# Down projection of a gated FFN: 8 of its 22 inner tiles as seven products over pairs of output tiles instead of eight

## The chip, the cores and the metric

One kernel runs on one core of a Trainium2 chip. The metric is the device time of one launch in microseconds (us). The core has five engines with a queue each: PE (matrix products, with its weight loads shown as PEld), DVE and ACT (element-wise work), POOL and SP (which here issues most transfers). Each engine works through its own queue in order; they wait for each other by semaphores.

## The reference, cut to what matters

The reference is one layer of a hybrid decoder: three gated token mixers, then a ConvFFN, over 1024 prompt tokens and 32 sample tokens, all float32. Only its last product is changed:

```
up = rmsnorm(x, g_pre_f) @ w_up                        # 1024 -> 2 x 2816
fa, fb = split(causal_dwconv(up, ffn_prev, conv_f_w, conv_f_b))
x = x + rmsnorm((silu(fa) * fb) @ w_down, g_post_f)    # 2816 -> 1024
```

`w_down` has 2816 rows, which are 22 inner tiles of 128, and 1024 columns, which are 8 output tiles of 128.

## The kernel before, in words

Everything is held transposed: a tile has 128 features on the partitions and the T = 1056 tokens along the free axis. A float32 operand is split into a high part (rounded to the PE's float32r type, by a copy on ACT, L91) and a low part (the rest, by a subtraction on DVE, L97). A product of two such operands takes three PE passes: high by high, high by low, low by high (`mm`, L100). So an inner tile times an output tile costs three passes for each chunk of tokens.

**The plain scheme** (`products`, L195). For an output tile, up to four inner tiles are multiplied for three chunks of 352 tokens; each chunk accumulates in one of five PSUM banks that are taken in turn (three called mm, two called wb), and is then evacuated. With four inner tiles that is 3 chunks x 4 tiles x 3 passes = 36 passes of 352 columns.

**The seven-product scheme** (`strassen`, L229, after Strassen and Winograd) is there already, for most of the up projection (j = 3 to 20) and for the gates. A pair of output tiles by eight inner tiles is a 2 x 2 block product: the inner tiles are two halves of four, and the tokens are two halves of 528, each again cut so that the parts p = 0, 1 pair columns of 264. Seven products of four inner tiles (names "11", "21", "T2", "T1", "T3", "T4", "22") take the place of eight; each is 2 parts x 4 tiles x 3 passes = 24 passes of 264 columns, so a pair has 168. The left operands are sums of weight blocks, made on DVE by `add_pair` (L169: four additions, L94, and seven splits). The right operands are sums of activation blocks, which have to be made once and are then used for all pairs. The products accumulate in banks called mm (X), wb (W) and aux (V).

**The down projection** comes last. The activations silu(fa) * fb are stored by tile to DRAM (`y2d`) as the up projection makes them, and come back by `load_y` (L1162): one transfer of 528 KB into the low slot, a copy on ACT into the high slot, a subtraction on DVE. Their slots are rows of Y and H, two large buffers of 16 rows each; until the down projection H holds the right operand of the up projection and Y its sums. The list `DOWN` (L33) cuts inner tiles 0 to 15 into four segments of four; `down` (L1168) runs a segment as eight plain units, one for each output tile, and adds into M (the first segment copies, on ACT; the later ones add, on DVE). After each unit it can load one more activation tile. Inner tiles 16 to 21 (`LAST` = 16 on) are done in a last stage by token chunks, which the final norm follows; that stage is not touched.

**Weights.** Every block of 128 x 512 weights is one transfer into a `raw` buffer (three of them), then a split into `wh` and `wl` (three each, so a split waits until PE is done with the split three before it). `make` keeps this three items ahead of PE, `load` four. In the pair scheme the blocks go to `xraw` buffers, which during the up projection are pieces of M.

**What sets the order.** PE's instructions stand in the order in which the program is written. In the down projection the other engines' queues are laid out by a scheduler that simulates the program, so their order is not in the source.

Of the kernel before, what the change touches and what calls it, by code (L numbers as in the profile page):

```python
# [9 lines left out]
F32 = mybir.dt.float32  # L10
F32R = mybir.dt.float32r
AF = mybir.ActivationFunctionType
ALU = mybir.AluOpType
# [4 lines left out]
P = 128  # L18
# [3 lines left out]
T = SEQ + NS  # L22
# [3 lines left out]
NFF = 22  # L26
# [3 lines left out]
NEG = -1e30  # L30
SCALE = 0.125
LAST = 16
DOWN = [(0, 4), (4, 8), (8, 12), (12, 16)]  # L33
PLAIN = 3
NC1 = 8 * 4 + 6 + 32 + 8 + 2
NCST = NC1 + 132 + 44
# [3 lines left out]
def body(tc, i, o):  # L40
    nc = tc.nc
    act, dve, pool, pe = nc.scalar, nc.vector, nc.gpsimd, nc.tensor
    top = ExitStack()
    with top, tc.manual_schedule(engines={mybir.EngineType.PE}):
        open_pool = lambda st, name, **kw: st.enter_context(tc.tile_pool(name=name, **kw))
# [12 lines left out]
        Y = fixed.tile([P, 16, T], F32R, name="Y")  # L58
        M = fixed.tile([P, 8 * T], F32, name="M")
        M8 = M.rearrange("p (k t) -> p k t", k=8)  # L60
        Yf = Y.rearrange("p s t -> p (s t)")
        x2d = dram.tile([P, 8, T], F32, name="x2d")
        y2d = dram.tile([P, NFF, T], F32, name="y2d")
# [20 lines left out]
        def cc(c):  # L84
            return slice(c * CW, (c + 1) * CW)

        def f32(ap):
            return ap.bitcast(F32)

        def copy(out, in_):  # L90
            act.activation(out, in_, AF.Copy)  # L91

        def tt(out, a, b, op, eng=dve):
            return eng.tensor_tensor(out, a, b, op=op)  # L94

        def sub(out, a, b, eng=dve):
            eng.tensor_tensor(out, a, b, op=ALU.subtract)  # L97
# [24 lines left out]
        xraw, limit = [None], [1 << 30]  # L122
# [33 lines left out]
        def add(src, nk, eng, where=None):  # L156
            for k0 in range(0, nk, 4):
                n = min(4, nk - k0)
                at = len(loads)
                loads.append((src[:, k0 : k0 + n, :], n, False))  # L160

                def fn(at=at, n=n, k0=k0):
                    raw, raws[at] = raws[at], None
                    to = where() if callable(where) else where
                    return split(raw, n, to and [t[:, k0 : k0 + n, :] for t in to], eng)

                items.append((at, n, fn))
# [54 lines left out]
        HC = 264  # L222

        def halves(p):

            one, two = ((0, 1), (3, 2))[p]
            return slice(one * HC, (one + 1) * HC), slice(two * HC, (two + 1) * HC)
# [49 lines left out]
        def unit(*args, **kw):  # L277
            for _ in products(*args, **kw):
                pass
# [77 lines left out]
        for j in range(2, NFF):  # L357
# [2 lines left out]
                continue  # L360
            for part in range(2):
                add(i["wu"][j + NFF * part], 8, dve)
        for g0, g1 in DOWN:
            for n in range(8):
                add(i["wd"][n, :, g0:g1, :], g1 - g0, dve)
        lastw = len(items)
        Hf = H.rearrange("p s t -> p (s t)")
        nl = (NFF - LAST) * P
        rest_of = [Yf[:, 12 * T + nl * q :][:, :nl] for q in range(5)] + [Hf[:, nl * q :][:, :nl] for q in range(11)]
        for n in range(8):  # L370
            add(i["wd"][n, :, LAST:NFF, :], NFF - LAST, dve,
                [rest_of[2 * n + h].rearrange("p (k m) -> p k m", m=P) for h in range(2)])
# [654 lines left out]
        with us:  # L1027
# [70 lines left out]
            def act_pair(j):  # L1098
                za = conv(*tile_of(j, 0))
                zb = conv(*tile_of(j, 1))  # L1100
                act.activation(za, za, AF.Silu)
                tt(za[:, :SEQ], za[:, :SEQ], zb[:, :SEQ], ALU.mult)
                tt(four(za[:, SEQ:T]), rest(za), rest(zb), ALU.mult)
                nc.scalar.dma_start(y2d[:, j, :], za[:, :T])
# [47 lines left out]
                    pass  # L1152
                act_pair(j)

            slots = [(Y[:, k], Y[:, 4 + k]) for k in range(4)]
            slots += [(Y[:, 8 + k], Y[:, 12 + k]) for k in range(4)]
            slots += [(H[:, k], H[:, 4 + k]) for k in range(4)]
            slots += [(H[:, 8 + k], H[:, 12 + k]) for k in range(4)]
            slots += [(Y[:, k], Y[:, 6 + k]) for k in range(6)]
            act_slot = lambda k: slots[k]  # L1160

            def load_y(k):  # L1162
                h, l = slots[k]
                nc.sync.dma_start(f32(l), y2d[:, k, :])
                copy(h, f32(l))
                sub(l, f32(l), f32(h))

            def down(k0, k1, then):  # L1168
                then = iter(then)
                for n in range(8):  # L1170
                    def evac_d(c, ps):
                        m = M8[:, n, cc(c)]
                        if k0 == 0:
                            copy(m, ps)
                        else:
                            tt(m, ps, m, ALU.add)
                    unit(k1 - k0, lambda k: act_slot(k0 + k)[0], lambda k: act_slot(k0 + k)[1], evac_d)
                    for k in [k for k in [next(then, None)] if k is not None]:
                        load_y(k)

            j = NFF - 1
            for part in range(2):
                for q, _ in enumerate(up_unit(j, part, CHUNKS)):
                    if not part and q < 4:
                        load_y(q)
            act_pair(j)
            nc.sync.dma_start(o["fx"], fx)
        for (k0, k1), then in zip(DOWN, (range(4, 8), range(8, 12), range(12, 16), range(16, 22))):
            down(k0, k1, then)


        with tc.tile_pool(name="pl", bufs=1) as pl:
# [162 lines left out]
```

## Time and profile before

| | |
|---|---|
| three timed runs | 1462.86 us median (1462.71 to 1464.74) |
| the profiled execution | 1468.9 us; its span, first to last instruction, 1467.1 us |
| PE's busy share of the span | 98% |
| DVE, ACT, POOL | 61%, 45%, 16% |
| mean granted PE clock | 0.987 |

The page's slices show PE at nine tenths or more from the second to the second-last slice. A busy PE says little alone, because passes overlap and their ends are modelled; what a pass costs is read from the distance between starts.

### The profile page before, as it was taken

Reading aid. Unit: us, or ns where it says so; the run is one execution under the profiler, and the core shown is the slowest. Engines: PE = TensorE matmul, PEld = TensorE weight load, DVE = VectorE, ACT = ScalarE, POOL = GpSimd, SP = SyncE. Lnnn points to the kernel's source line nnn. Section 1 sums busy time; section 2 is a strip of 40 time slices with the busy share of each in tenths; the row PEclk is TensorE's granted clock in tenths of the full one; section 3 lists DMA queues with packets and bytes.
Section 4 is the critical chain, followed back from the end, with each engine's and each line's share of the span. In section 5 each row is a group of like instructions: output and inputs, shape, how many; then the busy total and the mean of one; then the engine's idle time right before and its main releaser. Section 6 shows DMA issues by size and latency. Waiting matters only on the chain.

```text
span 1467.1 us, 25813 instructions
## 1 busy us (share of the span) xinstructions
PE 1438.9 (98%) x10211; PEld 1428.3 (97%) x10211; DVE 901.2 (61%) x1623; ACT 659.4 (45%) x1346; POOL 235.2 (16%) x319
## 2 busy tenths in 40 slices
PE   7999999999999999999999999999999999999997
PEld 7999999999999989999999999999999999999997
DVE  6665444325777546755678787777877782454546
ACT  6344444445766322243446455445544574121333
POOL 0000000013455215510002221222212210000000
PEclk7999999999999999999999999999999999999998
DMA  5223233211111136642232312222222274231215
GB/s 196 93 96 110 97 102 103 100 48 37 30 30 37 60 119 210 192 159 84 83 111 73 102 66 74 81 87 83 65 79 74 78 258 141 72 103 45 86 42 151
DMA packets 77817, 141.40 MB, mean 96 GB/s; under 512 B 8240, under 2 KB 34800, under 8 KB 77680
## 3 DMA queue, kind: packets, MB, share of 16 engines
q1 hardware_dynamic: 64256, 110.05, 23.8%
q10 hardware_dynamic: 13440, 29.70, 5.4%
q8 instruction: 80, 1.31, 0.4%
q14 instruction: 41, 0.34, 0.1%
HBM read 105.58 MB, written 35.16 MB: 96 GB/s over the span
## 4 chain that ended last, share of the span: by engine, by line
PE 91%; DVE 4%; ACT 2%; issue 2%; DMA 1%; SPq 0%; POOL 0%; ACTq 0%; POOLq 0%; DVEq 0%
PE mm L100 55%; PE wb L100 21%; PE aux L100 13%; DVE M L94 1%; PE sp L100 1%; ACT M L731 1%; PE aux L744 1%; DVE Y L97 1%; DVE M L416 1%; DVE M L725 0%; DMA M<-in_x 0%; DVE H L97 0%; DMA cst<-in_cst 0%; DVE M L604 0%; ACT Y L91 0%
## 5 line engine op out<-in xcount | busy, mean ns | idle before, releaser
L100 PE MATMUL mm<-Y,wh 128*128 128x264 f32 (+1 forms) x1824 | 363.8, 294 | 0.0
L100 PE MATMUL mm<-H,wh 128*128 128x352 f32 (+1 forms) x1568 | 354.4, 313 | 1.5 <-DVE Y L97 0.9
L100 PEld LDWEIGHTS mm<-Y,wh 128*128 128x128 f32 x1824 | 292.4, 188 | 0.0
L100 PE MATMUL mm<-Y,wl 128*128 128x264 f32 (+1 forms) x912 | 269.1, 295 | 0.0
L100 PEld LDWEIGHTS mm<-H,wh 128*128 128x128 f32 x1568 | 261.4, 188 | 2.5 <-PE aux L100 1.1
L100 PE MATMUL mm<-H,wl 128*128 128x352 f32 (+1 forms) x784 | 243.4, 311 | 0.0
L100 PEld LDWEIGHTS mm<-Y,wl 128*128 128x128 f32 x912 | 171.6, 188 | 0.0
L91 ACT ACTIVATE wh<-M 128x512 fp32r<-128x512 f32 x126 | 79.5, 631 | 152.8 <-PE aux L100 67.6
L100 PE MATMUL wb<-H,wh 128*128 128x264 f32 (+1 forms) x720 | 147.7, 298 | 0.0
L100 PEld LDWEIGHTS mm<-H,wl 128*128 128x128 f32 x784 | 147.2, 188 | 0.0
L91 ACT ACTIVATE wh<-raw 128x512 fp32r<-128x512 f32 (+1 forms) x98 | 58.2, 595 | 170.8 <-PE mm L100 111.7
L1092 DVE SCALAR_TENSOR_TENSOR cz<-U,cst,cz 128x1072 f32<-128x1072 f32 x88 | 113.7, 1329 | 10.9 <-ACT cz L1090 10.9
L100 PEld LDWEIGHTS wb<-H,wh 128*128 128x128 f32 x720 | 116.4, 188 | 0.0
L100 PE MATMUL mm<-H,Y 128*128 128x352 f32 x624 | 108.7, 333 | 1.0 <-DVE H L97 0.9
L100 PE MATMUL wb<-H,wl 128*128 128x264 f32 (+1 forms) x360 | 107.2, 298 | 0.0
L97 DVE TENSOR_TENSOR wl<-M,wh 128x512 fp32r<-128x512 f32 x126 | 86.3, 685 | 33.0 <-ACT wh L91 32.9
L100 PEld LDWEIGHTS mm<-H,Y 128*128 128x128 f32 x624 | 104.1, 194 | 2.1 <-DVE H L97 1.5
L97 DVE TENSOR_TENSOR wl<-xraw,wh 128x512 fp32r<-128x512 f32 x70 | 48.4, 692 | 80.6 <-ACT wh L91 80.2
L94 DVE TENSOR_TENSOR M<-M 128x512 f32<-128x512 f32 (+1 forms) x88 | 69.5, 789 | 27.8 <-DMA M<-in_wu 27.1
L94 DVE TENSOR_TENSOR M<-mm,M 128x352 f32<-128x352 f32 (+3 forms) x79 | 39.5, 505 | 76.6 <-PE mm L100 76.5
L97 DVE TENSOR_TENSOR wl<-raw,wh 128x512 fp32r<-128x512 f32 (+1 forms) x72 | 52.3, 729 | 51.9 <-ACT wh L91 51.9
L91 ACT ACTIVATE U<-mm 128x264 f32<-128x264 f32 (+4 forms) x199 | 63.8, 342 | 44.9 <-PE mm L100 42.5
(222 smaller groups left out, 2598.1 us busy)
## 6 DMA issues: line engine op xcount, KB each, us to landing
M<-in_wu SPq DMA_DIRECT2D x72, 256.0 KB, 2.6
sig<-sigd SPq DMA_DIRECT2D x72, 176.0 KB, 3.1
y2d<-cz ACTq DMA_DIRECT2D x22, 528.0 KB, 2.9
sigd<-M ACTq DMA_DIRECT2D x40, 264.0 KB, 2.2
xraw<-in_win SPq DMA_DIRECT2D x40, 256.0 KB, 2.9
raw<-in_wd SPq DMA_DIRECT2D x40, 256.0 KB, 2.6
raw<-in_win SPq DMA_DIRECT2D x39, 256.0 KB, 2.6
Y<-y2d SPq DMA_DIRECT2D x14, 528.0 KB, 5.6
```

Source lines behind the costliest of these rows:

```text
L91: act.activation(out, in_, AF.Copy)
L94: return eng.tensor_tensor(out, a, b, op=op)
L97: eng.tensor_tensor(out, a, b, op=ALU.subtract)
L100: pe.matmul(out, lhsT, rhs, start=start, stop=stop, skip_group_check=more)
L416: dve.scalar_tensor_tensor(m, m, g_pre[:, k : k + 1], R[:, cc(c)], ALU.mult, ALU.mult)
L731: act.activation(s[:, h, :], s[:, h, :], AF.Exp, bias=ng[:, h : h + 1], scale=SCALE, accum_out=l[:, h : h + 1])
L744: pe.transpose(pt[:, h * P : (h + 1) * P], s[:, h, kb * P : (kb + 1) * P], ident)
L1092: dve.scalar_tensor_tensor(z, u[:, s : s + CONV], cwf[:, f, s : s + 1], z, ALU.mult, ALU.add)
```

## The change

Of inner tiles 0 to 15, tiles 0 to 3 stay plain (`MID` = 4), tiles 4 to 11 become four pairs of output tiles in the seven-product scheme, and tiles 12 to 15 stay plain. The right operands of the pairs are made while the first plain segment runs:

- `load_b` brings activation blocks of four inner tiles by 264 tokens from `y2d` (four for p = 0 during the last up unit, four for p = 1 after the first down unit), 528 KB each, in runs of 1056 bytes.
- `blocks(p)` makes the seven right operands of a part: four subtractions of 128 x 1056 into buffers z, and seven splits (a copy on ACT and a subtraction on DVE, 128 x 1056 each). `prepare` calls one third of a part after each of the first six units.
- The high and low rows lie in Y, H and four new tiles e0 to e3; the z buffers, and after them seven `xraw` buffers for the weights of the pairs, lie in memory that the up projection has left.
- `evac_pair_d` adds each product from PSUM into M, on DVE, 264 columns at a time.
- The tiles that follow are loaded during the pairs: 12 to 15 into the slots of 0 to 3; 16 to 21 into rows of H, which until then hold right operands of the pairs.

```
--- before.py
+++ after.py
@@ -30,7 +30,7 @@
 NEG = -1e30
 SCALE = 0.125
 LAST = 16
-DOWN = [(0, 4), (4, 8), (8, 12), (12, 16)]
+MID = 4
 PLAIN = 3
 NC1 = 8 * 4 + 6 + 32 + 8 + 2
 NCST = NC1 + 132 + 44
@@ -360,13 +360,16 @@
                 continue
             for part in range(2):
                 add(i["wu"][j + NFF * part], 8, dve)
-        for g0, g1 in DOWN:
-            for n in range(8):
-                add(i["wd"][n, :, g0:g1, :], g1 - g0, dve)
+        for n in range(8):
+            add(i["wd"][n, :, 0:MID, :], MID, dve)
+        for n in range(0, 8, 2):
+            add_pair(*(i["wd"][m, :, MID : MID + 8, :] for m in (n, n + 1)))
+        for n in range(8):
+            add(i["wd"][n, :, MID + 8 : LAST, :], LAST - MID - 8, dve)
         lastw = len(items)
         Hf = H.rearrange("p s t -> p (s t)")
         nl = (NFF - LAST) * P
-        rest_of = [Yf[:, 12 * T + nl * q :][:, :nl] for q in range(5)] + [Hf[:, nl * q :][:, :nl] for q in range(11)]
+        rest_of = [Hf[:, 12 * T + nl * q :][:, :nl] for q in range(5)] + [Yf[:, 8 * T + nl * q :][:, :nl] for q in range(11)]
         for n in range(8):
             add(i["wd"][n, :, LAST:NFF, :], NFF - LAST, dve,
                 [rest_of[2 * n + h].rearrange("p (k m) -> p k m", m=P) for h in range(2)])
@@ -1152,11 +1155,9 @@
                     pass
                 act_pair(j)
 
-            slots = [(Y[:, k], Y[:, 4 + k]) for k in range(4)]
-            slots += [(Y[:, 8 + k], Y[:, 12 + k]) for k in range(4)]
-            slots += [(H[:, k], H[:, 4 + k]) for k in range(4)]
-            slots += [(H[:, 8 + k], H[:, 12 + k]) for k in range(4)]
-            slots += [(Y[:, k], Y[:, 6 + k]) for k in range(6)]
+            xraw[0] = None
+            slots = {k: (Y[:, k % 4], Y[:, 4 + k % 4]) for k in (*range(MID), *range(MID + 8, LAST))}
+            slots.update({LAST + k: (H[:, k], H[:, 6 + k]) for k in range(NFF - LAST)})
             act_slot = lambda k: slots[k]
 
             def load_y(k):
@@ -1165,28 +1166,109 @@
                 copy(h, f32(l))
                 sub(l, f32(l), f32(h))
 
-            def down(k0, k1, then):
-                then = iter(then)
-                for n in range(8):
-                    def evac_d(c, ps):
-                        m = M8[:, n, cc(c)]
-                        if k0 == 0:
-                            copy(m, ps)
-                        else:
-                            tt(m, ps, m, ALU.add)
-                    unit(k1 - k0, lambda k: act_slot(k0 + k)[0], lambda k: act_slot(k0 + k)[1], evac_d)
-                    for k in [k for k in [next(then, None)] if k is not None]:
-                        load_y(k)
+
+            NAMES = ("11", "21", "T2", "T1", "T3", "T4", "22")
+            rows = {}
+            for q, name in enumerate(NAMES):
+                rows[name, 0] = (H[:, q], Y[:, 8 + q])
+                rows[name, 1] = ((Y[:, 15], H[:, 14], H[:, 15], None, None, None, None)[q], H[:, 7 + q])
+
+            def block(name, h, p):
+                return rows[name, p][h].rearrange("p (k t) -> p k t", k=4)
+
+            def load_b(name, p):
+                r, cs = {"11": (0, 0), "T3": (0, 1), "22": (1, 1), "21": (1, 0)}[name]
+                nc.sync.dma_start(f32(block(name, 1, p)), y2d[:, MID + 4 * r : MID + 4 * r + 4, halves(p)[cs]])
+
+            def split_b(name, p, z=None):
+                h, l = block(name, 0, p), block(name, 1, p)
+                z = f32(l) if z is None else z
+                copy(h, z)
+                sub(l, z, f32(h))
 
             j = NFF - 1
             for part in range(2):
                 for q, _ in enumerate(up_unit(j, part, CHUNKS)):
                     if not part and q < 4:
                         load_y(q)
+                    if part and q < 4:
+                        load_b(("11", "T3", "22", "21")[q], 0)
             act_pair(j)
             nc.sync.dma_start(o["fx"], fx)
-        for (k0, k1), then in zip(DOWN, (range(4, 8), range(8, 12), range(12, 16), range(16, 22))):
-            down(k0, k1, then)
+
+        def down(k0, k1, then):
+            for n in range(8):
+                def evac_d(c, ps):
+                    m = M8[:, n, cc(c)]
+                    if k0 == 0:
+                        copy(m, ps)
+                    else:
+                        tt(m, ps, m, ALU.add)
+                unit(k1 - k0, lambda k: act_slot(k0 + k)[0], lambda k: act_slot(k0 + k)[1], evac_d)
+                then(n)
+
+        def evac_pair_d(n):
+            held = {}
+
+            def f(q, p, t):
+                one, two = halves(p)
+                c11, c12, c21, c22 = (M8[:, r, cs] for r in (n, n + 1) for cs in (one, two))
+                if q == 3:
+                    held[p] = t
+                    return
+                to = (c11, c11, c12, None, c22, c21, c12)[q]
+                tt(to, t, to, ALU.add)
+                if q == 4:
+                    tt(c22, held[p], c22, ALU.add)
+            return f
+
+        with tc.tile_pool(name="dn", bufs=1, reuse_waits="tile") as dn:
+            for q, name in enumerate(NAMES[3:]):
+                rows[name, 1] = (dn.tile([P, T], F32R, name=f"e{q}"), rows[name, 1][1])
+            dz = ExitStack()
+            zs = open_pool(dz, "dz", bufs=3, reuse_waits="tile")
+
+            def blocks(p):
+                raw = lambda name: f32(block(name, 1, p))
+
+                def made_of(name, a, b):
+                    z = zs.tile([P, 4, HC], F32, name="z")
+                    sub(z, a, b)
+                    split_b(name, p, z)
+                    return z
+
+                z = made_of("T1", raw("T3"), raw("11"))
+                split_b("11", p)
+                yield
+                z = made_of("T2", raw("22"), z)
+                made_of("T4", raw("21"), z)
+                split_b("21", p)
+                yield
+                made_of("T3", raw("22"), raw("T3"))
+                split_b("22", p)
+                yield
+
+            def prepare(n):
+                if n == 0:
+                    for name in ("11", "T3", "22", "21"):
+                        load_b(name, 1)
+                next(both, None)
+                if n == 5:
+                    dz.close()
+                    xraw[0] = dz.enter_context(tc.tile_pool(name="dx", bufs=7, reuse_waits="tile"))
+
+            both = (None for p in range(2) for _ in blocks(p))
+            down(0, MID, prepare)
+
+            def Bd(name, k, p):
+                return tuple(block(name, h, p)[:, k, :] for h in range(2))
+
+            for n in range(0, 8, 2):
+                for q, _ in enumerate(strassen(Bd, new, evac_pair_d(n))):
+                    if q == 3:
+                        load_y(MID + 8 + n // 2)
+            dz.close()
+        down(MID + 8, LAST, lambda n: load_y(LAST + n) if n < NFF - LAST else None)
 
 
         with tc.tile_pool(name="pl", bufs=1) as pl:
```

How the queues of DVE and ACT change is shown at three places. The names: wh and wl are a weight's high and low part, M the accumulator, z the sums of activation blocks, e0 to e3 (with a number) the new tiles.

**ACT at the start of the first down segment**, from the evacuation of the last up unit on, before:

```order
L91 ACTIVATE U_7988<-wb 128x8x4
L1090 ACTIVATE cz<-U_7988,cst 128x1072
L91 ACTIVATE H<-H 128x1056
L91 ACTIVATE M<-mm 128x352
L91 ACTIVATE H<-H 128x1056
L91 ACTIVATE M<-mm 128x352
```

and now:

```order
L91 ACTIVATE M<-mm 128x352
L1093 ACTIVATE cz<-U_7988,cst 128x1072
L91 ACTIVATE Y<-H 128x1056
L91 ACTIVATE M<-mm 128x352
L91 ACTIVATE wh<-raw 128x512
L91 ACTIVATE M<-mm 128x352
L91 ACTIVATE M<-wb 128x352
L1107 DMA y2d<-cz 128x1056
L91 ACTIVATE M<-wb 128x352
L91 ACTIVATE wh<-raw 128x512
L91 ACTIVATE M<-mm 128x352
L91 ACTIVATE e_13301<-H 128x1056
```

The copies of activation tiles between the evacuations have become copies of blocks: Y<-H and e_13301<-H need blocks of p = 1 that have just been loaded.

**DVE in the same segment**, from the convolution of the last up tile on, before:

```order
L1092 SCALAR_TENSOR_TENSOR cz<-U_7988,cst,cz 128x1072
L97 TENSOR_TENSOR H<-H 128x1056 x2
L94 TENSOR_TENSOR cz<-cz 128x1024
L94 TENSOR_TENSOR cz<-cz 128x32
L97 TENSOR_TENSOR wl<-raw,wh 128x512
L97 TENSOR_TENSOR H<-H 128x1056 x3
L97 TENSOR_TENSOR wl<-raw,wh 128x512
```

and now, the beginning of the block work and its end at the first pair:

```order
L94 TENSOR_TENSOR cz<-cz 128x1024
L94 TENSOR_TENSOR cz<-cz 128x32
L97 TENSOR_TENSOR wl<-raw,wh 128x512
L97 TENSOR_TENSOR z<-Y 128x1056
L97 TENSOR_TENSOR Y<-Y,H 128x1056
L97 TENSOR_TENSOR z<-Y,z 128x1056
```

with twenty rows of this kind between, and then

```order
L97 TENSOR_TENSOR H<-H,e_13301 128x1056
L97 TENSOR_TENSOR H<-z,e_13299 128x1056
L97 TENSOR_TENSOR wl<-xraw,wh 128x512 x2
L94 TENSOR_TENSOR xraw<-xraw 128x512
L94 TENSOR_TENSOR M<-mm,M 128x264
L94 TENSOR_TENSOR xraw<-xraw 128x512 x2
L94 TENSOR_TENSOR M<-mm,M 128x264
L94 TENSOR_TENSOR xraw<-xraw 128x512
L97 TENSOR_TENSOR wl<-xraw,wh 128x512
```

The block work (22 subtractions, with three splits of plain weights among them) stands as one stretch behind the fifth plain weight's split, and ahead of the splits of the first pair's weights.

**DVE where tiles 16 to 21 are split**, before, for four of them:

```order
L94 TENSOR_TENSOR M<-wb,M 128x352
L97 TENSOR_TENSOR Y<-Y 128x1056
L94 TENSOR_TENSOR M<-wb,M 128x352
L97 TENSOR_TENSOR Y<-Y 128x1056
L94 TENSOR_TENSOR M<-mm,M 128x352
L97 TENSOR_TENSOR Y<-Y 128x1056
L97 TENSOR_TENSOR wl<-raw,wh 128x512
```

and now, in the last pair:

```order
L97 TENSOR_TENSOR H<-H 128x1056
L94 TENSOR_TENSOR M<-mm,M 128x264
L97 TENSOR_TENSOR wl<-xraw,wh 128x512
L94 TENSOR_TENSOR M<-mm,M 128x264
L97 TENSOR_TENSOR H<-H 128x1056
L97 TENSOR_TENSOR wl<-xraw,wh 128x512
L97 TENSOR_TENSOR H<-H 128x1056
L94 TENSOR_TENSOR M<-mm,M 128x264
L97 TENSOR_TENSOR wl<-xraw,wh 128x512
L94 TENSOR_TENSOR M<-aux,M 128x264
```

Here each H<-H waits for a transfer into a row of H that the pair's products read until just before, and the evacuations and weight splits of the pair stand behind it.

## Rows read from the trace of the kernel before

**Rows 1.** The page: busy time by engine, and the chain's shares by engine

```profile
PE 1438.9 (98%) x10211; PEld 1428.3 (97%) x10211; DVE 901.2 (61%) x1623; ACT 659.4 (45%) x1346; POOL 235.2 (16%) x319
...
PE 91%; DVE 4%; ACT 2%; issue 2%; DMA 1%; SPq 0%; POOL 0%; ACTq 0%; POOLq 0%; DVEq 0%
```

**Rows 2.** Waits of PE, 720 to 1440 us: in total, times, longest (us)

```profile
PE aux L100 <- DVE acc L94: 1.8, 1, 1.8
```

**Rows 3.** Chain of waits, up to down projection: start us, us, what, passes

```profile
1091.63 2.93 PE aux L100 x24
...
1173.58 2.93 PE aux L100 x24
1176.51 1.92 PE wb L100 x12
...
1199.42 5.76 PE mm L100 x36
...
1247.42 5.76 PE mm L100 x36
...
1339.39 3.82 PE wb L100 x24
```

**Rows 4.** Busy time by engine, DMA share, GB/s, in stretches of us

```profile
790.00:1170.00 380.00, 380.00 (x3085) 380.00 (x3084) 292.09 (x440) 192.50 (x369) 78.00 (x112) 1.00 0.22 74
1199.40:1245.50 46.10, 46.10 (x291) 46.10 (x290) 18.70 (x20) 24.13 (x43) 0.52 (x2) 1.00 0.55 194
...
1202.00:1206.00 4.00, 4.00 (x27) 4.00 (x27) 4.00 (x4) 4.00 (x7) 0.00 (x0) 1.00 1.05 386
```

**Rows 5.** Groups of DVE and ACT: xcount, busy us, mean ns, idle before

```profile
L94 DVE TENSOR_TENSOR M<-M 128x512 f32<-128x512 f32 x72 | 49.4, 686 | 27.7 <-DMA M<-in_wu 27.1
L97 DVE TENSOR_TENSOR wl<-xraw,wh 128x512 fp32r<-128x512 f32 x70 | 48.4, 692 | 80.6 <-ACT wh L91 80.2
...
L94 DVE TENSOR_TENSOR M<-aux,M 128x264 f32<-128x264 f32 x40 | 17.2, 429 | 7.6 <-PE aux L100 6.9 <-ACT M L91 0.7
...
L97 DVE TENSOR_TENSOR H<-H 128x1056 fp32r<-128x1056 f32 x8 | 9.8, 1250 | 0.8 <-ACT H L91 0.8
...
L91 ACT ACTIVATE wh<-xraw 128x512 fp32r<-128x512 f32 x70 | 44.1, 629 | 60.0 <-PE mm L100 19.9 <-PE aux L100 19.9 <-PE wb L100 18.1
...
L91 ACT ACTIVATE Y<-Y 128x1056 fp32r<-128x1056 f32 x14 | 14.9, 1081 | 6.1 <-DMA Y<-y2d 6.1
...
L91 ACT ACTIVATE M<-wb 128x352 f32<-128x352 f32 x9 | 4.1, 454 | 5.1 <-PE wb L100 5.1
```

**Rows 6.** Timeline of DVE and ACT in the first down segment

```profile
1207.76 1.31 DVE L94 TENSOR_TENSOR cz<-cz 128x1024 f32<-128x1024 f32 x2
1209.00 0.68 DVE L97 TENSOR_TENSOR wl<-raw,wh 128x512 fp32r<-128x512 f32 x1
1209.60 3.58 DVE L97 TENSOR_TENSOR H<-H 128x1056 fp32r<-128x1056 f32 x3
...
1211.39 0.63 ACT L91 ACTIVATE wh<-raw 128x512 fp32r<-128x512 f32 x1
```

**Rows 7.** Timeline: issues of activation tiles by SP, and the first copy behind each

```profile
1197.86 2.99 SPq L1164 DMA_DIRECT2D H<-y2d  x6
...
1244.89 0.81 SPq L1164 DMA_DIRECT2D Y<-y2d  x2
...
1248.27 1.08 ACT L91 ACTIVATE Y<-Y 128x1056 fp32r<-128x1056 f32 x1 [1.91 <-DMA Y<-y2d]
...
1290.17 1.76 SPq L1164 DMA_DIRECT2D Y<-y2d  x4
...
1293.82 1.09 ACT L91 ACTIVATE Y<-Y 128x1056 fp32r<-128x1056 f32 x1 [1.74 <-DMA Y<-y2d]
```

**Rows 8.** Transfers: landing of y2d tiles; of sig (352 columns); of weights, 1245 to 1300 us

```profile
DMA to landing us min/median/max: 2.7/4.0/11.8
...
DMA to landing us min/median/max: 2.3/3.1/7.9
...
raw<-in_wd SPq DMA_DIRECT2D x9, 256.0 KB, 2.6
```

**Rows 9.** Weight loads in the up projection's pairs and, on the last line, in the down segments

```profile
L100 PEld LDWEIGHTS mm<-Y,wh 128*128 128x128 f32 x832 | 129.3, 188 | 0.0
...
L100 PEld LDWEIGHTS mm<-Y,wh 128*128 128x128 f32 x240 | 41.7, 188 | 0.0
```

## The prediction

> **What bounds the kernel now.** I read the page first: PE is busy 98% of the span and carries 91% of the chain, DVE is at 61% and ACT at 45% [rows 1]. Then the waits of PE from the up projection on: between 720 and 1440 us there is one, of 1.8 us, at the very start of that stretch [rows 2]. It covers all 18 pairs of the up projection, which are in the seven-product scheme, and all four plain segments of the down projection. So in the changed stretch the time is the number of passes times their spacing, and nothing else ends a wait. The chain gives the spacing [rows 3]. The reader is to see that a product of 24 passes of 264 columns starts every 2.93 us, and that the starts 1091.63 and 1173.58 are four whole pairs apart, 672 passes in 81.95 us, 121.9 ns each. Between 1247.42 and 1339.39 the plain chunks stand as ten pieces of 36 passes and nine of 24, 576 passes of 352 columns in 91.97 us, 159.7 ns each. The clock is at its full level in all these stretches [rows 4].
>
> **The passes.** Inner tiles 4 to 11 are two plain segments before: 2 x 8 units x 36 = 576 passes, 92.0 us. Afterwards they are four pairs: 4 x 168 = 672 passes of 264 columns, 82.0 us by the pairs of the up projection, which have the same shape, banks and order. That is 10.0 us less. The other segments and the last stage keep their passes. The trace shows that PE waits for nobody there, so what is taken from PE comes off the end, less the waits that the change brings. These I look for at three places. The first plain segment starts at 1199.42 and lasts 288 x 159.7 ns = 46.0 us, to 1245.4.
>
> On a pass's price the Trainium skill (TensorE: Matmul & The Clock Gate, section Back-to-back issue gap) speaks against the change: for a real stream of weight loads and matmuls it gives about 81 ns at 128 columns and 131 ns at 512, so a pass's price would hang little on its length. A straight line through these, an estimate, is 99 ns at 264 columns and 110 ns at 352: 66.3 us for the pairs against 63.5 us for the plain units, 2.8 us slower. The rows differ in level and in slope, and the measurement decides.
>
> **Place 1: the block operands, on DVE and ACT.** They replace the eight activation tiles that were split in the same segment and before it. New on DVE are 8 sums and 14 low parts, all 128 x 1056. The trace has such subtractions at 1.25 us, and three in a row in 3.58 us, so 1.19 us each [rows 5, 6]. The stretch stands behind the fifth plain weight's split, whose high part cannot be made before PE has finished the second unit (1199.4 + 11.5; the same copy starts at 1211.39 in the trace) [rows 6], so it begins about 1212.7; the convolution ahead of it ended at about 1209 before, with three tile splits among it that now go. 22 x 1.19 + 3 weight splits x 0.6 = 28.0 us, which ends at 1240.7. PE's first pair comes at 1245.4: 4.7 us to spare. In total DVE has 18.7 us of work in this segment before [rows 4], of which the eight tile splits (9.8) [rows 5] go; with 27.5 us of block work it is some 36 of 46. ACT makes 14 copies of 1.08 us more, 15 us, on top of its 24.1 us, of which eight copies of activation tiles go: about 31 of 46. All this lies beside PE. If DVE's cover were gone, the excess would be paid in full: at 1.6 us an operation 22 x 0.41 = 9.0 us more, less the spare 4.3 us. I take nothing, since these are operations that the trace shows in the same shape and memory.
>
> The block transfers are as many bytes as the eight tile loads they replace, in runs of 1056 bytes. Those of p = 0 share the queue with tiles 0 to 3, during the last up units, where the eight tiles went before.
>
> **Place 2: the first pair's weights.** They are new in kind: their buffers lie on the z buffers, so the transfers wait until the last sums are split, 1236 to 1240.7. One lands 2.6 us after its issue [rows 8]; six at 386 GB/s, the rate of a full stretch [rows 4], are 4.1 us together, so the first are there by 1243.5 and four by 1245. On ACT the first high part stands behind the evacuation of the last unit's second chunk (1243.5 + 0.45), then 0.63 for the copy and 0.69 for the low part [rows 5]: 1245.3, against 1245.4. For the third product DVE then does another low part, four additions of 0.69, two evacuations of 0.43 and a low part, with PE's first two chunks between: 1250.3, wanted at 1251.2. So from nothing to about 1 us; I take 0.2, since each step ends before its time, by little. Within the pairs DVE has 7 x 0.69 + 4 x 0.69 + 14 x 0.43 = 13.6 us for 20.5 us; in the up pairs it has 292/380 of that time, 15.8 us [rows 4], and PE never waited. So the steady state costs nothing.
>
> **Place 3: the tiles 16 to 21 in the last pair.** Each is loaded into a row that a product has just released, and DVE's subtraction for it (H<-H) stands ahead of evacuations. From issue to the first copy the trace shows 3.4 and 3.7 us (1244.89 to 1248.27, 1290.17 to 1293.82) [rows 7]; then 1.08 us for the copy and 1.25 for the subtraction, so it ends 5.9 us after the product that released the row. The third such row is released when the third product ends. Behind its subtraction on DVE stands the evacuation of the fifth product's first part (0.43), and the sixth product wants that bank 2 x 2.93 = 5.86 us after the release. So 0.5 us is missing; with the transfers' median of 4.0 us [rows 8] it is 1.0, and if each landed at 5 us about 1.8. The lower bound is 0.3, since 2.7 us is the shortest landing but the others share the queue. I take 0.5, the nearer rows. The segment behind it (tiles 12 to 15) and the last stage have their inputs as early as before.
>
> **Sum.** -10.0 + 0.2 + 0.5 = -9.3 us. The profiled execution took 1468.9 us and would take 1459.6. It stands 0.4% over the median of the runs, 1462.86; 9.3 us at that scale stays 9.3: 1453.6 us.
>
> **The rivals.** *Larger waits at the two seams.* For it: places 2 and 3 have under 1 us to spare, and DVE and ACT work in strict order, so one late transfer holds up the evacuations behind it. Landings of the y2d tiles reach 11.8 us where many are queued [rows 8]. Against: at both seams the queue holds only few transfers. Waits of 3 to 7 us would leave a gain of 3 to 7: 1456 to 1460. At the upper end this is no change.
>
> *ACT held up by the block loads, to a loss.* The copy Y<-H stands on ACT behind the first evacuation of the segment and waits for a block of p = 1 that can only be asked for at about 1199. All later evacuations stand behind it, and e_13301<-H, four evacuations on, waits for another block. PE goes on while the five banks last: chunks 2 to 6 fill by 1199.4 + 6 x 1.92 = 1210.9. The four blocks are 2.16 MB, at 386 GB/s 5.6 us and some 2 us to land: 1207, in time. At half that rate the first still lands in time. The second copy comes four chunks, 7.7 us, later, so it has until 1217, and PE loses its 10 us only if that block lands at 1227 or later, which is 2.16 MB in 27 us, 80 GB/s. From there on the change is a loss: at 60 GB/s the block lands at 1237, PE waits 20 us, and the time is 1473. The shortest runs in the trace, 352 columns, land in 3.1 us for 176 KB [rows 8], which speaks against it.
>
> *Passes spaced by their weight loads.* Each pass has a load of 188 ns, the same at both lengths [rows 9], and there are 96 more. If these loads set the spacing, 96 x 159.7 ns = 15.3 us would be added: 1478. But passes start 121.9 ns apart, under the load's own time, so loads overlap, and the spacing follows the columns (37.8 ns for 88 columns). The estimate from the skill's figures would come out on this side too, by 2.8 us, for 1465.7; the rows leave both next to nothing.
>
> *The change doesn't do what it says:* the order on PE is written out, and the queue shows the pairs' weights and evacuations, so I leave it no chance of its own.
>
> **How the numbers follow.** What a measurement of this kernel can tell from no change is about 0.2%, 2.9 us. The forecast, a gain of 6.5 to 10.5 us (1452.4 to 1456.4), has 0.77; larger waits with a gain that still shows 0.10; waits that eat it up to no change 0.08; the hold-up on ACT 0.04; the weight loads 0.01. So faster 0.87, within 0.2% 0.08, slower 0.05. The time is 1453.6. The range goes from 1451.8 (no wait at all, and the scatter of the runs) to 1458.0, which takes in the upper bounds of both seams together and half of the larger waits.
>
> **What would show it.** In the changed profile: 672 passes of 264 columns in the down projection at 2.93 us a product, and four pairs in 82 us; the last block subtraction (H<-z,e) at least 3 us before the first pair; waits of PE of under 1 us at the first pair and of about 0.5 us around the sixth product of the last pair, and none in the pairs between; the last stage starting about 9.3 us earlier. I am wrong if PE waits in the first plain segment, if a product takes more than 3 us, or if the waits at the seams come to more than 3 us.

## The result, and the profile after

The changed kernel takes 1455.49 us (median of 6 runs, 1453.04 to 1460.19) beside 1465.51 us for the kernel before (6 runs, 1462.71 to 1467.62): ratio 0.9933, interval 0.9917 to 0.995, so 9.8 us less (7.3 to 12.2). The forecast was 9.3 us less. Its time, 1453.6 us, was reckoned from a median of three runs, 1462.86; the six runs of the kernel before have a median 2.65 us higher, and for that alone the forecast time is 1.9 us too low. The profiled execution took 1460.19 us, its span 1458.5.

The page of the changed kernel, busy time by engine, beside the first line of [rows 1]:

```profile
PE 1429.8 (98%) x10307; PEld 1418.9 (97%) x10307; DVE 932.3 (64%) x1673; ACT 672.1 (46%) x1364; POOL 232.6 (16%) x319
```

PE has 96 passes more and 9.1 us less work, and its share of the span is as it was. Its waits between 720 and 1440 us (total, times, longest), which answer to [rows 2]:

```profile
PE aux L100 <- DVE acc L94: 1.7, 1, 1.7
PE mm L100 <- DVE M L94: 0.3, 1, 0.3
```

The first line was there before. The second is the only wait that the change brings. The chain of waits of the changed kernel (start us, us, what), beside [rows 3]:

```profile
1199.64 5.76 PE mm L100 x36
...
1245.72 2.92 PE mm L100 x24
...
1266.19 2.92 PE mm L100 x24
...
1307.13 2.92 PE mm L100 x24
...
1312.96 2.85 PE mm L100 x24
1315.81 3.30 DMA H<-y2d
...
1319.20 1.09 ACT H L91
...
1320.32 1.26 DVE H L97
1321.58 0.35 DVE M L94
1321.93 0.14 issue
1322.07 3.17 PE mm L100 x24
...
1328.15 1.92 PE wb L100 x12
1330.08 5.76 PE mm L100 x36
...
1374.23 6.56 PE wb L100 x36
...
1432.25 0.64 PE aux L100 x8
```

The reader is to see four pairs, of which the second and the fourth start 2 x 20.47 us apart, and a break in the last: there the chain leaves PE for a transfer, a copy, a subtraction (H) and the evacuation behind it (M), and comes back at the sixth product, 1322.07. The four pairs run from 1245.72 to 1328.15, 82.43 us. The last PE piece of the last stage stands at 1432.25, where in the kernel before it was this:

```profile
1441.34 0.64 PE aux L100 x8
```

It comes 9.1 us earlier now, though the first segment began 0.22 us later. From the start of that segment to this piece it is 232.61 us, after 241.92: 9.3 us less. The experiments are compared by this stretch (called the stretch from here on), since PE's work ahead of it is the same in all kernels here.

### The profile page after: what moved, and what is told of

Same layout as the page of the kernel before. It is cut to its first block, busy times and chain, and to the rows that moved or that the text cites. A ratio compares the mean times of both kernels' runs of the same rounds, so it can differ in the third digit from the quotient of the medians.

```text
span 1458.5 us, 26087 instructions
## 1 busy us (share of the span) xinstructions
PE 1429.8 (98%) x10307; PEld 1418.9 (97%) x10307; DVE 932.3 (64%) x1673; ACT 672.1 (46%) x1364; POOL 232.6 (16%) x319
## 4 chain that ended last, share of the span: by engine, by line
PE 91%; DVE 4%; ACT 2%; issue 2%; DMA 1%; SPq 0%; POOL 0%; ACTq 0%; POOLq 0%; DVEq 0%
PE mm L100 55%; PE wb L100 19%; PE aux L100 15%; DVE M L94 1%; PE sp L100 1%; ACT M L734 1%; PE aux L747 1%; DVE Y L97 1%; DVE M L419 1%; DVE H L97 0%; DVE M L728 0%; DMA M<-in_x 0%; DMA cst<-in_cst 0%; SPq L379 0%; DVE M L607 0%
## 5 line engine op out<-in xcount | busy, mean ns | idle before, releaser
L100 PE MATMUL mm<-Y,wh 128*128 128x264 f32 (+1 forms) x1904 | 386.4, 294 | 0.0
L100 PE MATMUL mm<-H,Y 128*128 128x352 f32 (+2 forms) x798 | 139.3, 331 | 1.0 <-DVE H L97 0.9
L100 PEld LDWEIGHTS mm<-H,Y 128*128 128x128 f32 x798 | 132.5, 193 | 2.1 <-DVE H L97 1.5
L97 DVE TENSOR_TENSOR wl<-xraw,wh 128x512 fp32r<-128x512 f32 x98 | 67.7, 691 | 91.8 <-ACT wh L91 90.5
L100 PE MATMUL wb<-H,wh 128*128 128x264 f32 (+1 forms) x608 | 119.9, 291 | 0.0
L91 ACT ACTIVATE wh<-xraw 128x512 fp32r<-128x512 f32 x98 | 61.5, 629 | 105.8 <-PE mm L100 45.2
L100 PE MATMUL aux<-H,wh 128*128 128x264 f32 x512 | 101.4, 285 | 0.0
L100 PEld LDWEIGHTS wb<-H,wh 128*128 128x128 f32 x608 | 96.7, 188 | 0.0
L100 PE MATMUL aux<-Y,wh 128*128 128x264 f32 x480 | 92.4, 285 | 0.0
L100 PE MATMUL wb<-H,Y 128*128 128x352 f32 (+2 forms) x498 | 89.4, 337 | 0.0
```

The source lines that it names most:

```text
L100: pe.matmul(out, lhsT, rhs, start=start, stop=stop, skip_group_check=more)
```

## The experiments

Each ratio is to the kernel before, timed beside it (medians 1464.59, 1465.75 and 1464.72 us in the three sets).

**Pass price alone.** The kernel before, with its tiles 4 to 11 still in plain units, but in four chunks of 264 columns:

```
+    quarter = 4 <= k0 < 12
+    cols = (lambda c: slice(c * HC, (c + 1) * HC)) if quarter else cc
-    unit(k1 - k0, ..., evac_d)
+    unit(k1 - k0, ..., evac_d, range(4) if quarter else CHUNKS, cols)
```

> The kernel before, with the two plain segments of inner tiles 4 to 11 cut into four chunks of 264 tokens instead of three of 352: no seven products, the same columns in 768 passes instead of 576. Theory (a pass costs 121.9 ns at 264 columns and 159.7 at 352, as the pairs and the plain units show): 768 x 121.9 = 93.6 us against 92.0, the run 1.6 us slower than before, a unit of 48 passes 5.85 us. Rival, passes spaced by their weight loads: 192 more passes x 159.7 ns, 31 us slower. The straight line through the figures of the Trainium skill (TensorE: Matmul & The Clock Gate, section Back-to-back issue gap), an estimate of 99 ns at 264 columns and 110 at 352: a unit of 4.74 us against 5.29, 12 us slower.

Measured: ratio 1.0017 (1.0005 to 1.0029), 2.5 us more (0.7 to 4.2); the stretch is 243.27 us, 1.35 more than before, against 1.6 expected. Its chain:

```profile
1251.68 4.38 PE mm L100 x36
1256.06 2.92 PE wb L100 x24
...
1336.26 3.82 PE wb L100 x24
```

60 passes take 7.30 us, 121.7 ns each, in plain units too. All 768 take 93.3 us (1242.93 to 1336.26), 121.5 ns each, where 576 of 352 columns took 92.0 [rows 3]. So the price follows the columns: 88 columns more cost 38 ns, 0.43 ns each, which leaves 7 to 8 ns on top in every pass. 192 passes more, each with its weight load, cost 1.35 us in all. A price set by the loads (31 us more) falls. So does one by the Trainium skill's figures for streams (TensorE: Matmul & The Clock Gate, section Back-to-back issue gap), an estimate of 12 us more. (The 5.29 us of that estimate is a slip: a unit of 352 columns has 36 passes, 3.97 us at 110 ns each, and from there come the 12 us.)

**Half the dose.** Output tiles 0 to 3 as two pairs, 4 to 7 as plain units:

```
-            for n in range(0, 8, 2):
+            for n in (0, 2):
...
+        for n in range(4, 8):
+            unit(8, lambda k: act_slot(MID + 8 + k % 4)[0], ..., evac_x)
```

> The changed kernel with half the dose: output tiles 0 to 3 in two pairs, output tiles 4 to 7 plain for inner tiles 4 to 11. The right operands are all made as before. The plain units read the slots of inner tiles 12 to 15 twice in place of 4 to 11, so the output is not the reference's. Theory (the gain is the passes, 2.5 us for each pair, and the block work costs nothing): 4.7 us faster than the kernel before, 5.0 us slower than the changed one, no wait of PE over 0.5 us. Rival, block work or its transfers cost a fixed amount that the pairs pay back: then half the pairs leave less than half of the gain, down to none.

Measured: ratio 0.9985 (0.9974 to 0.9996), 2.2 us less (0.6 to 3.8): a miss. The stretch is 3.0 us shorter, not 4.7. The waits of PE there:

```profile
PE mm L100 <- DVE M L94: 1.2, 2, 0.7
```

The two pairs take 42.66 us (1244.36 to 1287.02), 1.7 more than 2 x 20.47. One wait is the seam at the last pair, the other is new, in the first pair. I first blamed the tile loads, of which two stand in each pair in the program, and spread them (these lines change the run above; its plain units now also read the pairs' rows of Y and H, not the slots of tiles 12 to 15):

```
-                    if q in (3, 7):
-                        load_y(MID + 8 + n + (q == 7))
+                    if q == 3:
+                        load_y(MID + 8 + n // 2)
+            if n in (4, 6):
+                load_y(MID + 8 + n // 2)
```

> Output tiles 0 to 3 as two pairs in the seven-product scheme, output tiles 4 to 7 as plain units, as in the earlier run with two pairs, but the loads and splits of tiles 12 to 15 are spread as in the changed kernel: one in each pair and the other two behind plain units (the plain units read operands of the pairs in place of tiles 4 to 11, so the output is not the reference's). Half of the change: 288 plain passes of 352 columns and 336 of 264, so the passes alone are 5.0 us less than before. Theory: the earlier run gained only 2.2 us because two tile splits stood in each pair, and waits of PE of 1.2 us came of it; with them spread PE has waits under 0.5 us in this stretch, and the time is 4.5 to 5.0 us below the kernel before, ratio 0.9966 to 0.9970. Rival (a fixed cost of 2 to 3 us comes with the scheme however many pairs there are, for instance at its first pair): the trace has no larger waits than 0.5 us either, yet the two pairs take over 42 us, and the time is again about 2 us below the kernel before.

Measured: ratio 0.9979 (0.9967 to 0.9992), 3.1 us less (1.2 to 4.8), one wait of 0.5, the pairs 41.68 us, the stretch 3.6 us shorter. That is short of the 4.5 to 5.0 us expected. The seam at the last pair was gone, the wait in the first pair was not. Spreading the loads did not take the seam away: the plain units now read the high rows of H behind the pairs, so the copies into them come later. The transfers are still issued in the last pair (from 1268.20 on), but the first subtraction H<-H stands at 1326.66, 41 us behind the pairs' end, where the run above had it at 1273.32, in the last pair. Why the first pair waits is shown by DVE's timeline there, for the changed kernel (pair from 1245.72):

```profile
1257.37 1.25 DVE L97 TENSOR_TENSOR Y<-Y 128x1056 fp32r<-128x1056 f32 x1
1258.54 0.69 DVE L97 TENSOR_TENSOR wl<-xraw,wh 128x512 fp32r<-128x512 f32 x1
1259.14 0.43 DVE L94 TENSOR_TENSOR M<-mm,M 128x264 f32<-128x264 f32 x1
```

and for the first run with two pairs (pair from 1244.36):

```profile
1255.93 0.69 DVE L94 TENSOR_TENSOR xraw<-xraw 128x512 f32<-128x512 f32 x1
1256.53 1.25 DVE L97 TENSOR_TENSOR Y<-Y 128x1056 fp32r<-128x1056 f32 x1
1257.70 0.69 DVE L97 TENSOR_TENSOR wl<-xraw,wh 128x512 fp32r<-128x512 f32 x1
1258.30 0.69 DVE L94 TENSOR_TENSOR xraw<-xraw 128x512 f32<-128x512 f32 x1
1258.90 0.77 DVE L94 TENSOR_TENSOR M<-mm,M 128x264 f32<-128x264 f32 x2
```

In these two kernels and in the spread run the scheduler puts the four splits of tiles 12 to 15 (Y<-Y) into the first pair, wherever the program loads them. My reason for the miss was wrong. With two pairs it also draws two weight sums (xraw) ahead of the evacuation, so this begins 14.54 us after the pair's start, not 13.42 (the text below has 13.33), and the sixth product, due at 14.6, waits. To test it, the subtractions were held, and the loads of tiles 12 to 15 moved in the program behind the plain units:

```
+                if k >= MID + 8:
+                    with tc.issue_after(last_pair[0]):
+                        sub(l, f32(l), f32(h))
```

> Two pairs and four plain output tiles again, as in the run with the spread loads, but all of DVE's subtractions for the tiles behind the pairs (12 to 21) are held until the last pair's last evacuation (the plain units still read operands of the pairs in place of tiles 4 to 11, so the output is not the reference's). In the runs with two pairs the scheduler had put all four splits of tiles 12 to 15 into the first pair, and one weight sum more ahead of them than in the changed kernel, so an evacuation began 14.54 us after the pair's start instead of 13.33, and the sixth product waited. Theory: without them there is no wait of PE, two pairs take 40.94 us (half of 81.89), and from the first segment's start to the last pass of the last stage it is 4.1 to 4.6 us less than before (5.04 for the passes, less 0.3 to 0.9 for plain passes that run up to 1% slower than before); by the times 4 to 5 us below the kernel before, ratio 0.9965 to 0.9973. Rival (a fixed cost of the scheme): two pairs take over 41.5 us, or the stretch is less than 3.7 us shorter, with no wait in the trace.

Measured: ratio 0.9961 (0.9946 to 0.9975), 5.7 us less (3.7 to 7.9); PE waits for nothing between 1190 and 1440 us. The chain:

```profile
1199.91 5.76 PE mm L100 x36
...
1245.99 2.92 PE mm L100 x24
...
1286.93 1.94 PE wb L100 x12
...
1294.68 5.81 PE mm L100 x36
...
1437.48 0.64 PE aux L100 x8
```

Two pairs take 40.94 us, and the stretch is 4.35 us shorter, as expected. The two weight sums stand ahead of the evacuation here too, and with no split among them nothing waits. So half the pairs take half the time of four; the stretch falls short of the passes' 5.04 us by 0.7, since the plain units take 5.81 us here (see the last section). There is no fixed cost that the trace shows. The miss was DVE's order in one pair.

**No block work.** The changed kernel without the block loads, sums and splits; the pairs read other rows of Y and H:

```
-                    if part and q < 4:
-                        load_b(("11", "T3", "22", "21")[q], 0)
...
-                    for name in ("11", "T3", "22", "21"):
-                        load_b(name, 1)
-                next(both, None)
```

> The changed kernel without the block work: no block transfers, no sums, no splits of right operands; the pairs read what the rows hold, and the four new tiles are replaced by rows of Y, so the output is not the reference's. Theory (all of it lies beside PE): the same time as the changed kernel within 0.5 us, 9.5 to 10 us faster than before, with the same wait of 0.3 us in the last pair; in the first plain segment DVE is near idle and the pairs' weights are there early. Rival, the block work costs part of the gain through ACT, DVE or the transfers: several us faster than the changed kernel, up to 1450.

Measured: ratio 0.9949 (0.9931 to 0.9968), 7.5 us less than before (4.7 to 10.1), so no faster than the changed kernel; 9.5 to 10 were expected. The stretch is 233.15 us, 0.54 more than in the changed kernel: the wait in the last pair is 0.7 us here, and the other three pairs take 20.53 us each, with other rows read. The first segment in the windows view (PE, PEld, DVE, ACT, POOL busy, clock, DMA, GB/s), this run first, then the changed kernel, which answers to the second line of [rows 4]:

```profile
1198.40:1244.40 46.00, 46.00 (x290) 46.00 (x289) 12.22 (x16) 16.40 (x35) 0.52 (x2) 1.00 0.29 92
```

```profile
1199.60:1245.70 46.10, 46.10 (x291) 46.10 (x290) 34.45 (x34) 27.56 (x46) 0.52 (x2) 1.00 0.36 113
```

In this segment 22 us of DVE and 11 us of ACT go, and PE's 46.0 us stay. The work is hidden whole, within the 0.5 us by which the stretches differ.

**The cover used up.** The eight sums made twice:

```
                     sub(z, a, b)
+                    sub(z, a, b)
```

> The changed kernel with each of the eight sums of activation blocks made twice (the second writes the same values): 8 x 1.17 = 9.4 us more on DVE in the first plain segment. In the changed kernel the last block subtraction ends at 1240.0, 5.7 us before the first pair. Theory (the cover is those 5.7 us and the excess is paid): the last sum ends at 1249.4, four tile splits that the scheduler now puts ahead of the first weights' low parts add up to 5 us, so PE waits 4 to 11 us at the first pair and the run takes 1458 to 1466, most or all of the gain gone. Rival (DVE's queue is no limit, since its share of the time is 64%): no wait of PE, the same time as the changed kernel.

Measured: ratio 1.0027 (1.0015 to 1.0039), 4 us slower than before (2.2 to 5.7), and 1467.59 us is past the expected 1458 to 1466. The stretch is 245.44 us, 12.8 more than in the changed kernel. The waits of PE from 1190 us on:

```profile
PE mm L100 <- ACT wh L91: 7.7, 1, 7.7
PE mm L100 <- DVE wl L97: 1.9, 1, 1.9
PE mm L100 <- DVE M L94: 0.5, 1, 0.5
```

The first two, 9.6 us, are at the first pair and lie in the range I gave. 8 x 1.17 = 9.4 us of DVE, less 5.7 us to spare, would make 4; but four tile splits (4.7 us) now stand ahead of the first weights, whose buffers come free late. Most of the rest is the clock (chain; then windows: PE busy, clock, DMA, GB/s):

```profile
1256.31 5.08 PE mm L100 x22
```

```profile
1245.90:1256.30 10.40, 0.81 (x2) 0.74 0.86 310
1256.30:1261.40 5.10, 5.09 (x24) 0.53 0.23 87
1261.40:1341.10 79.70, 79.17 (x649) 1.00 0.26 72
```

After PE had idled, its next 22 passes ran in 5.08 us, 231 ns each, at a granted clock of 0.53, near the lower level of 1.2 GHz; at 121.9 ns they would have taken 2.7, so this cost 2.4 us more. My theory had left that out.

**The seam taken away.** The changed kernel, with DVE's subtractions of tiles 16 to 21 held behind the last pair:

```
-                sub(l, f32(l), f32(h))
+                if k >= LAST:
+                    with tc.issue_after(last_pair[0]):
+                        sub(l, f32(l), f32(h))
+                else:
+                    sub(l, f32(l), f32(h))
...
-                tt(to, t, to, ALU.add)
+                last_pair[:] = [tt(to, t, to, ALU.add).ins]
```

> The changed kernel, with DVE's subtractions for tiles 16 to 21 (H<-H) held until the last pair's last evacuation, so that none stands ahead of an evacuation that PE waits for. Theory (the subtraction for the third such row stands ahead of the evacuation that frees the bank of the sixth product): PE's one wait in the last pair, 0.3 us in the changed kernel, is gone, the last pair takes 20.47 us like the three ahead of it, and the segment behind it still finds its tiles, since DVE has 46 us for six subtractions there. The time is about 0.3 us below the changed kernel's, too little for the times to tell, about 9.5 us below the kernel before. Rival A (PE waits there for the weights or for the transfer itself): the wait of 0.3 us stays. Rival B (the six subtractions then come too late for the last stage, or hold up the first evacuations of the segment behind): a new PE wait of 1 us or more behind 1328 us.

Measured: 1453.33 us, ratio 0.9911 (0.9897 to 0.9926), 13.0 us less (10.8 to 15.1) where about 9.5 was expected. PE has no wait between 1190 and 1440 us. The chain of its last pair, and DVE's subtractions behind it:

```profile
1301.22 2.92 PE mm L100 x24
...
1318.75 2.94 PE aux L100 x24
1321.69 1.92 PE wb L100 x12
```

```profile
1322.12 5.93 DVE L97 TENSOR_TENSOR H<-H 128x1056 fp32r<-128x1056 f32 x5
```

The last pair takes 20.47 us like the others. Four pairs are 81.89 us (from 1239.80), 0.54 less than in the changed kernel. Both rivals fall. This version beats both kernels in the trace; its times are better than 0.54 us explains, and the next run is there to tell what else is in them.

**The changed kernel again**, on the chip of the seam run:

> The changed kernel itself once more, beside the runs with part of it undone and on their chip, so that they can be compared. Theory: 9 to 10 us below the kernel before (ratio 0.9930 to 0.9940), the four pairs in 82.0 to 82.5 us, the only wait of PE in the down projection 0.3 to 0.5 us in the last pair. Rival (part of the gain belonged to the first measurement's scatter, as its runs lie 7 us apart): a gain under 7 us, ratio above 0.9952.

Measured: 1456.34 us, ratio 0.9936 (0.9919 to 0.9954), 9.4 us less (6.7 to 11.9), so by the times the rival's bound of 7 us is just inside the interval; the stretch is 9.0 us less than before. Its seam wait was 0.6 us and the pairs 82.75 us, both a little past what I gave. The 3 us between the medians of these two go with the clock. All five runs without the seam had a mean granted clock of 0.991 to 0.994, the six of this run 0.986 to 0.992. At 0.992 the changed kernel took 1454.6 and 1454.7 us; runs without the seam at 0.991 and 0.993 took 1453.3 to 1454.3. The stretch is 232.07 us without the seam and 232.93 with it, and that difference, 0.86 us, is what the traces support.

## Why the prediction was right

**The passes** (-10.0 us). Four pairs without a seam take 81.89 us, 672 passes of 121.9 ns, the price read from the up projection; the run on pass price (121.5 ns in plain units) and the two pairs of 40.94 us show that it depends little on the scheme and the stage.

**Place 1** (cost 0). The timeline of DVE, and ACT's copy Y<-H, in the changed kernel:

```profile
1211.70 0.69 DVE L97 TENSOR_TENSOR wl<-raw,wh 128x512 fp32r<-128x512 f32 x1 [3.40 <-ACT wh L91]
1212.31 1.25 DVE L97 TENSOR_TENSOR z<-Y 128x1056 f32<-128x1056 f32 x1
...
1238.77 1.26 DVE L97 TENSOR_TENSOR H<-z,e 128x1056 fp32r<-128x1056 f32 x1
1244.85 1.30 DVE L97 TENSOR_TENSOR wl<-xraw,wh 128x512 fp32r<-128x512 f32 x2 [4.81 <-ACT wh L91]
...
1250.00 0.69 DVE L97 TENSOR_TENSOR wl<-xraw,wh 128x512 fp32r<-128x512 f32 x1
```

```profile
1204.38 1.09 ACT L91 ACTIVATE Y<-H 128x1056 fp32r<-128x1056 f32 x1 [0.83 <-DMA H<-y2d]
```

The block work starts at 1212.3 (forecast 1212.7) and ends at 1240.0 (1240.7), 5.7 us ahead of the first pair. DVE has 34.5 us in the segment (36), ACT 27.6 (31). The run without block work shows the cost of nothing, the run with doubled sums that the cover is finite. The copy Y<-H, on which the rival of a hold-up rested, waited 0.83 us, to 1204.38; by the prediction's reckoning (1210.9 less the copy and an evacuation) it could have waited to 1209. The 1.6 us an operation with which the prediction prices a lost cover stand in no row and in no run: the subtractions took 1.25 us and started 1.17 us apart. Its 4.3 us of spare beside 4.7 is a slip; neither enters the sum.

**Place 2** (0.2). The cost was nothing. Two low parts begin at 1244.85, so the first, 0.69 us long, is there at 1245.5 for a pair that starts at 1245.72; the third ends at 1250.7 for a product at 1251.54. The margins, 0.2 and 0.8 us, are near those worked out, 0.1 and 0.9. One step of this part was wrong and did no harm: the 13.6 us of DVE's work in a pair leave out the tile splits. Four of them stand in the first pair, where DVE is busy 19.1 of 20.5 us, so that at the sixth product it is within 0.6 us of its limit (the evacuation ends 13.85 us after the pair's start, and the product is due at 14.6, 0.14 behind its release). That PE did not wait there was not worked out, so it was luck; the runs with two pairs fell over it.

**Place 3** (0.5). The wait is where it was put, at the sixth product of the last pair, behind the third subtraction H<-H and the evacuation behind it. It shows as 0.3 us (0.6 in the second profile), and the pairs lose 0.54 us (0.86). Holding the subtractions took it away, so the cause is shown. Its size goes with the landing of that transfer: over four profiles, 3.30, 3.52, 3.62 and 3.67 us in the chain gave waits of 0.3, 0.5, 0.6 and 0.7 us (the changed kernel, the doubled sums, the repeat, no block work). Of the other figures given there, the lower bound of 0.3 does not follow from a landing of 2.7 us (2.7 + 1.08 + 1.25 + 0.43 = 5.46, under 5.86, so no wait), and 4.0 us make 0.9; the 0.5 taken rests on neither.

**Not foreseen** (+0.24). The segment of tiles 12 to 15 takes 46.08 us (1328.15 to 1374.23), where the one that stood last before took 45.84 (9.55 us for each 60 of its 288 passes). By these parts the stretch is -10.03 + 0.54 + 0.24 = -9.25 us; measured it is -9.31, and the forecast was -9.3. Each size was off by no more than 0.3 us; that the total fits to a tenth is luck, since the 0.2 of place 2 that did not come and the 0.24 that did come cancel.

## What to carry to other kernels

Where one engine waits for nobody, a change of its instruction count is worth count times spacing, and the spacing can be read from another stage with the same shape (here to 0.1 us in 82). What is left to forecast are the seams: work out, for each bank or buffer handed over there, what stands ahead of the releasing instruction on its engine, since an average of 74% busy (60.7 of 82.4 us on DVE in the pairs) says nothing about the one product where four tile splits stand. Holding slow steps that nobody needed yet until the last evacuation took every wait out of the pairs here, which was worth 0.54 to 0.86 us.

## What the runs showed of the hardware

**Scatter comes from the clock in two places ahead of the change.** The windows view (PE busy, clock, DMA, GB/s) of the changed kernel, then of the one without the seam:

```profile
0.00:60.00 60.00, 50.16 (x282) 0.80 0.49 167
...
720.00:730.00 10.00, 9.09 (x46) 0.66 0.17 54
```

```profile
0.00:60.00 60.00, 50.05 (x299) 0.86 0.49 167
...
720.00:730.00 10.00, 10.00 (x65) 1.00 0.17 53
```

The two kernels have the same program up to here, and in both PE waited once for DVE near 720 us, 1.7 and 1.6 us. In the one the granted clock was 0.50, the lower level, from 722 to 728 us after that, in the other it did not fall. Of the ten profiles, eight show a fall there; the other one without is the repeat of the changed kernel, so it doesn't come from the seam. The first segment began at 1199.64 in the one and 1193.72 in the other: 5.9 us, over half of what the change is worth, 2.8 of them there by 717 us and 3.1 after. So the times alone tell little below 3 us, and the traces are to be compared by stretches.

**A pass's price went with the rows of its operand, by up to 1.4%.** In the kernel before, the third and fourth plain segments read rows of H, 5.73 us for 36 passes (its chain):

```profile
1333.66 5.73 PE mm L100 x36
```

The first two, and the last one of the changed kernel (1330.08, shown above), read rows of Y: 5.76 us. Units that mixed both in the held run took 5.81 (1294.68, shown above). The segment that stands last read H before and reads Y now, and 0.03 us for each 36 passes make the 0.24 us above. That the rows are the cause was not tested.
